# Experts of up to 32 rows on four column tiles of TensorE, their pairs in a chain of their own

## The chip, the cores and the metric

The kernel runs on 1 core of one Trainium2 chip. The metric is the device time of one execution in microseconds (us). Before the change it is 2599.8 us, the median of 3 runs (2597.35 to 2602.37).

## The reference, cut to what matters

Two transformer blocks run one after the other on 512 tokens of width 1024. The first holds differential attention, a gated linear recurrence and an MLP; the second holds sparse and forgetting attention and a mixture of 32 experts, of which each token takes four. The change is in the experts alone:

```
logits = (xf @ w_router + b_router).astype(jnp.float32)
top_v, top_i = lax.top_k(logits, TOP_K)
w = jax.nn.softmax(top_v, axis=-1)
...
sizes = jnp.bincount(flat_e, length=N_EXPERTS).astype(jnp.int32)
xs = xf[tok]
h = lax.ragged_dot(xs, w_up, sizes) + b_up[sorted_e]
g, lin = jnp.split(h, 2, axis=-1)
g = jnp.minimum(g, SWIGLU_LIMIT)
lin = jnp.clip(lin, -SWIGLU_LIMIT, SWIGLU_LIMIT)
act = g * jax.nn.sigmoid(SWIGLU_ALPHA * g) * (lin + 1.0)
y = lax.ragged_dot(act, w_down, sizes) + b_down[sorted_e]
y = y * w.reshape(-1)[order][:, None].astype(y.dtype)
return jax.ops.segment_sum(y, tok, num_segments=n).reshape(B, T, D)
```

An expert has 1024 x 2048 and 1024 x 1024 weights in fp32. With the reference's inputs the router gives the experts these numbers of rows, by size: 149, 143, 130, 127, 126, 121, 101, 101, 87, 87, 82, 74, then 63, 57, 53, 51, 45, 43, 43, 42, 40, 36, 33, and nine of 31, 30, 29, 29, 29, 26, 19, 12 and 9. The counts are known only at run time.

## The kernel before, in words

**Two ways to run an expert.** `expert` takes up to 128 rows: the rows and the weights are split into a high and a low part (`split`, ACT at L219 and DVE at L220), and TensorE multiplies three terms (`part`, bias at L1316, products at L1322). `few` takes up to 64 rows and multiplies fp32 weights as they come: `halves` cuts the 512 columns of a product into two halves that land on partitions 0 to 63 and 64 to 127 of one bank (biases L1517, products L1521). The rows are gathered by POOL (L1289), turned by TensorE (`flip`, L1303) and copied to `xf` by DVE (L1307) or split; the activation is `gated` (L1345 to L1349). In a few it is turned back at L1550 and copied at L1551 into `h`, which lies in the tile `y`. `finish` scales the result into the same tile `y` (ACT at L1364 for an expert; ACT at L1369 and DVE at L1370 for a few), and POOL adds it to the output by a scatter (L1293).

**The weights.** Each expert's weights are 12 chunks of 1 MB (`ORDER`: eight of w_up, four of w_dn), read by SP's queue (L1122) into a ring of eight buffers (`RAW`). A chunk's buffer is refilled with the chunk eight places on when it has been read: after the products in a few, after the split in an expert.

**The order at run time.** The experts are sorted by size on the chip (`order`) and their number and places are read from a table (`ovi`) by `load` (L1214). A pair is a small expert by `few` and then a big one by `expert`, so that the weights of one come while TensorE works at the other; the small ones are paired smallest first. `pairs` nests fifteen branches (L1235), each with one pair in it, and runs on to `rest`, which bisects (L1243, L1247) to the fews that have no big partner. There are 11 pairs with these inputs and then nine fews and one more. A branch not taken jumps over all the code of the deeper ones.

**The second rows.** In the first four pairs (`SECOND`) the big expert also runs its rows beyond 128, up to 32 of them, on four column tiles of 32 rows: `second_rows` turns them (L1459), `second` multiplies (biases L1476, products L1482). In those pairs the weights stay in the ring until both have read them.

In the expert the order of the work is written out as follows (`finish` is called by the expert for the few ahead of it):

```
for i in range(12):
    n = e * 12 + i
    if i < 10:
        self.split(*self.pairs[(n + 2) % self.PAIRS], self.raw(n + 2))
        ...
    self.part(bank(i), x if i < 8 else m["h"], i, self.pairs[n % self.PAIRS], one)
    if two:
        for k in range(i + (i > 0), min(i + 2, 12)):
            self.second(k, e)
            self.refill(e * 12 + k)
    if i == 0 and e:
        self.finish(e - 1, False)
```

The scheduler then sets the order on each engine's queue. Names of tiles: `lg` and `mm` are PSUM banks of the products, `pv` those of the second rows, `tr` of the transposes; `b` is any of several buffers, `wh` and `wl` the high and low part of a chunk.

Of the kernel before, what the change touches and what calls it, by code (L numbers as in the profile page):

```python
# [11 lines left out]
F32 = mybir.dt.float32  # L12
# [4 lines left out]
AF = mybir.ActivationFunctionType  # L17
OP = mybir.AluOpType
# [7 lines left out]
NE, TT = 32, 128  # L26
# [131 lines left out]
class K:  # L158
# [1050 lines left out]
    def places(self, srt):  # L1209

        tc, nc = self.tc, self.nc

        def load(i, n):
            return nc.values_load(self.ovi[0:1, i:i + 1], min_val=0, max_val=n, skip_runtime_bounds_check_because="a count")  # L1214

        plain = load(2, 1)
        with tc.If(plain > 0) as cmp:
            self.expert(0)
        with cmp.Else():
            kind, nfar = load(0, 1), load(7, 64)  # L1220
            with tc.If(kind > 0) as cm2:
                self.expert(0)
            with cm2.Else():
                self.few(0)
            with tc.If(nfar > 0):
                self.extra(srt)
                with tc.For_i(0, nfar, 1) as it:
                    er = nc.values_load(self.li[0:1, ds(it, 1)], engines=(mybir.EngineType.SP, mybir.EngineType.DVE),
                                        min_val=0, max_val=NE - 1, skip_runtime_bounds_check_because="an expert's number")
                    self.far(er, it)  # L1230
        nP = load(1, 15)

        def pairs(t):
            if t < NE // 2 - 1:
                with tc.If(nP > t):  # L1235
                    self.few(1 + 2 * t, True, t < self.SECOND)
                    self.expert(2 + 2 * t, t < self.SECOND)
                    pairs(t + 1)

        def rest(lo, hi):  # L1240
            if hi - lo > 1:
                mid = (lo + hi) // 2
                with tc.If(nP < mid):  # L1243
                    rest(lo, mid)
# [110 lines left out]
            return mm[(s + i // 2) % 4]  # L1355
        return mm[(s + i % 2) % 4]

    def finish(self, e, big):

        nc, m = self.nc, self.m  # L1360
        sl, i = m["sl"][e // 4 % 2], e % 4
        if big:
            for c in range(2):
                nc.scalar.activation(m["y"][0][:, 512 * c:512 * c + 512], self.bank(e, 8 + c), AF.Copy, scale=sl["w"][:, i:i + 1])  # L1364
            self.scatter(m["y"][0], sl, i)
        else:
            for c in range(2):
                p, w = self.bank(e, 8 + c), sl["w"][:64, i:i + 1]
                nc.scalar.activation(m["y"][0][:64, 512 * c:512 * c + 256], p[:64, :256], AF.Copy, scale=w)  # L1369
                nc.vector.tensor_scalar(m["y"][0][:64, 512 * c + 256:512 * c + 512], p[64:, :256], w, None, op0=OP.mult)  # L1370
            self.scatter(m["y"][0], sl, i, 64)

    def numbers(self, e):

# [41 lines left out]
    def expert(self, e, two=False):  # L1416

        nc, m = self.nc, self.m
        one, x, act = m["one"][e % 2], m["x"][e % 2], m["act"][0]
        bank = partial(self.bank, e)  # L1420
        self.numbers(e)
        if two:
            self.second_rows()
# [4 lines that stand above are left out]
                if not two:  # L1428
                    self.refill(n + 2)
            if i < 2 and not two:  # L1430
                self.refill(n)
# [13 lines left out]
        self.finish(e, True)  # L1445

    def cut(self, w, up, j, n, of):

# [56 lines left out]
    def halves(self, p, x, i, e):  # L1505
# [5 lines left out]
        o = p[:64, :256], p[64:, :256]  # L1511

        cut = lambda w, n: self.cut(w, up, j, n, 2)
        if up and kh == 0:
            b = self.bup.bitcast(F32)[:, 512 * (j // 2):512 * (j // 2) + 512]
            for n in range(2):
                nc.tensor.matmul(o[n], self.m["one"][e % 2].bitcast(F32)[:, j % 2, :64], cut(b, n), start=True, stop=False)  # L1517
        w = self.raw(e * 12 + i).rearrange("p (k f) -> p k f", k=4)
        for k in range(4):
            for n in range(2):  # L1520
                nc.tensor.matmul(o[n], x(4 * kh + k), cut(w[:, k], n), start=not up and kh == k == 0, stop=kh == 1 and k == 3)  # L1521

    def few(self, e, paired=False, second=False):

        nc, m = self.nc, self.m
        self.numbers(e)
        xf, act = m["xf"], m["act"][0][:, :512]
        hf = m["y"][0][:, :512].rearrange("p (t a r) -> p t a r", t=4, a=2)
        h = lambda k: hf[:, k % 2, k // 2] if k < 4 else hf[:, k % 2 + 2, k // 2 - 2]
        for i in range(12):  # L1530
            n = e * 12 + i
            self.halves(self.bank(e, i), (lambda k: xf[:, k]) if i < 8 else h, i, e)
            self.refill(n)
            if i > 9 and (paired or e == NE - 1):
                self.unfold(n + 2)
            if i == 0 and e and e % 2 == 0:
                self.finish(e - 1, False)
            self.ahead(e, i, 8, paired)
            if i == 3 and second:
                self.further(e + 1)  # L1540
            if i in (3, 5, 7):
                j = i // 2
                pg, pl = [self.bank(e, k)[:, :256] for k in (0, 2)] if j == 1 else \
                    [self.bank(e, i)[:, 128 * k:128 * k + 128] for k in range(2)]
                self.gated(pg, pl, self.side(act, j, 64))
            if i in (5, 8, 9):
                t0, t1 = {5: (0, 2), 8: (2, 3), 9: (3, 4)}[i]
                p = self.tr()
                for t in range(t0, t1):
                    nc.tensor.transpose(p[:, t - t0], act[:, 128 * t:128 * t + 128], self.ident)  # L1550
                nc.vector.tensor_copy(hf[:, t0:t1].rearrange("p t a r -> p t (a r)"), p[:, :t1 - t0])  # L1551
            if e == NE - 1 and i == 6:
                self.last_rows(e)
        if e % 2 == 0:
            self.finish(e, False)
        if e == NE - 1:
            self.last(e)

# [176 lines left out]
    def order(self, c):  # L1735


        nc, m, ones = self.nc, self.m, self.c["ones"]
# [10 lines left out]
        gt = S2[:, 160:222].rearrange("p (a e) -> p a e", a=2)  # L1749
        col = [S2[:, 284 + i:285 + i] for i in range(12)]  # L1750
        kc, big, q1, g, sb, far, ex = col[:7]
        r4 = S2[:, 296:298]
        r, na = [r4[:, i:i + 1] for i in range(2)]
# [45 lines left out]
        v.memset(of[:, 3:7], 0.0)  # L1799
# [139 lines left out]
```

## Time and profile before

| what | value |
| --- | --- |
| time, median of 3 runs | 2599.8 us (2597.35 to 2602.37) |
| profiled execution, its own time | 2600.15 us |
| its span | 2598.1 us (2.05 us lie around it) |
| mean granted TensorE clock | 0.972 |
| PE busy | 2425.4 us, 93% |
| DVE busy | 1326.2 us, 51% |
| ACT busy | 1043.5 us, 40% |
| POOL busy | 174.5 us, 7% |
| HBM read over the span | 530.03 MB |

The shares are averages over stages with different limits. The expert stage begins in the 22nd of the 40 slices and ends in the 39th. A window's line gives the busy time of each engine in it, the granted clock of TensorE as a share of full speed, and the mean busy share of the 16 DMA engines. In a timeline the bracket behind an instruction tells how long its engine was idle before it, and what released it; "q" behind an engine is its sequencer, which issues DMAs and runs branches.

### The profile page before, as it was taken

How to read it: one execution, taken by the hardware profiler on the slowest of the kernel's cores; microseconds unless marked ns; L12 is line 12 of the kernel's file. 1: busy time of each engine (PE TensorE's matmuls, PEld its weight loads, DVE VectorE, ACT ScalarE, POOL GpSimd, SP SyncE). 2: the span in 40 equal slices, each digit the busy share in tenths (PEclk: the TensorE clock that was granted, in tenths of full speed). 3: DMA queues.
4: the chain of work that ended last, by engine and by line, in shares of the span. 5: the costliest groups of instructions: out<-in, count | busy, mean ns of one | idle time of the engine just before them, and what ended most of it. 6: DMA issues, size and time to landing. Idle time of an engine off the chain costs nothing. (4 is left out here: it accounts for less than half of the span.)

```text
span 2598.1 us, 41846 instructions
## 1 busy us (share of the span) xinstructions
PE 2425.4 (93%) x17042; PEld 1941.2 (75%) x17042; DVE 1326.2 (51%) x2473; ACT 1043.5 (40%) x1578; POOL 174.5 (7%) x184
## 2 busy tenths in 40 slices
PE   7999999999999999999989999999999999788888
PEld 5789987898898898898976676666666666554557
DVE  6767753344333344557585466445656666121135
ACT  5755552223223324557353344334444444111133
POOL 0021100000000000000010010110001000000000
PEclk9999999999999999999979999999999999899999
DMA  4122222322222222220378889989999999799990
GB/s 160 65 90 78 74 70 89 127 86 88 98 93 86 98 70 83 75 71 17 109 271 324 305 317 333 341 301 367 381 378 392 385 403 373 294 399 400 407 376 33
DMA packets 86474, 552.63 MB, mean 213 GB/s; under 512 B 11799, under 2 KB 12951, under 8 KB 24936
## 3 DMA queue, kind: packets, MB, share of 16 engines
q1 hardware_dynamic: 71280, 508.33, 50.6%
q0 software_dynamic: 8352, 29.76, 4.7%
q10 hardware_dynamic: 6616, 11.53, 1.3%
q8 instruction: 142, 2.33, 0.4%
q14 instruction: 84, 0.69, 0.1%
HBM read 530.03 MB, written 19.55 MB: 212 GB/s over the span
## 5 line engine op out<-in xcount | busy, mean ns | idle before, releaser
L245 PE MATMUL mm<-b,wh 128*128 128x512 f32 (+1 forms) x1840 | 512.8, 365 | 1.7 <-ACT b L222 0.8
L245 PEld LDWEIGHTS mm<-b,wh 128*128 128x128 f32 x1840 | 328.8, 190 | 65.4 <-issue 3.4
L245 PE MATMUL mm<-b,wl 128*128 128x512 f32 (+2 forms) x920 | 335.2, 365 | 1.3 <-DVE wl L205 1.3
L245 PE MATMUL mm<-wh,b 128*128 128x256 f32 x1488 | 284.3, 287 | 1.5 <-DVE b L675 0.8
L205 DVE TENSOR_TENSOR wl<-raw,wh 128x2048 fp32r<-128x2048 f32 x81 | 185.5, 2290 | 176.2 <-ACT wh L204 176.2
L204 ACT ACTIVATE wh<-raw 128x2048 fp32r<-128x2048 f32 x81 | 155.1, 1915 | 261.2 <-PE mm L245 248.8
L245 PEld LDWEIGHTS mm<-wh,b 128*128 128x128 f32 x1488 | 235.9, 191 | 4.6 <-DVE b L675 1.2
L245 PE MATMUL mm<-wl,b 128*128 128x256 f32 x744 | 213.0, 286 | 1.0 <-DVE wl L205 1.0
L220 DVE TENSOR_TENSOR wl<-b,wh 128x2048 fp32r<-128x2048 f32 x74 | 169.2, 2288 | 65.4 <-ACT wh L219 62.4
L245 PEld LDWEIGHTS mm<-b,wl 128*128 128x128 f32 (+1 forms) x920 | 174.6, 190 | 31.8 <-DVE wl L205 2.2
L1521 PE MATMUL lg<-b,xf 128*64 128x256 f32 x1280 | 154.3, 389 | 14.7 <-DMA b<-w_up 10.1
L219 ACT ACTIVATE wh<-b 128x2048 fp32r<-128x2048 f32 x74 | 141.0, 1908 | 61.8 <-DMA b<-w_up 30.8
L245 PEld LDWEIGHTS mm<-wl,b 128*128 128x128 f32 x744 | 141.9, 191 | 2.5 <-DVE wl L205 1.3
L1521 PEld LDWEIGHTS lg<-b,xf 128*64 128x64 f32 x1280 | 94.3, 139 | 65.7 <-DMA b<-w_up 15.9
L1521 PE MATMUL lg<-b,b 128*64 128x256 f32 x1024 | 130.7, 394 | 7.5 <-DMA b<-w_dn 7.2
L213 POOL TENSOR_TENSOR rs<-rm,c_nhalf 128x1 f32<-128x1 f32 (+3 forms) x52 | 53.0, 1021 | 1158.9 <-DVE rm L211 1150.6
L1521 PEld LDWEIGHTS lg<-b,b 128*64 128x64 f32 x1024 | 76.0, 141 | 49.1 <-issue 11.5
L1345 ACT ACTIVATE sg<-mm,seven 128x128 f32<-128x128 f32 (+2 forms) x48 | 21.8, 455 | 223.2 <-PE mm L1521 180.9
L1521 PE MATMUL mm<-pp,xf 128*64 128x256 f32 x640 | 84.3, 388 | 4.6 <-DMA pp<-w_up 4.5
L1347 DVE SCALAR_TENSOR_TENSOR sg<-lg,sg 128x256 f32<-128x256 f32 (+1 forms) x48 | 19.2, 399 | 127.6 <-ACT sg L1346 127.6
L1521 PE MATMUL mm<-b,xf 128*64 128x256 f32 x640 | 74.8, 383 | 7.0 <-DMA b<-w_up 7.0
L1345 ACT ACTIVATE sg<-lg,seven 128x256 f32<-128x256 f32 (+1 forms) x48 | 21.7, 452 | 146.1 <-PE lg L1521 118.4
(534 smaller groups left out, 4597.9 us busy)
## 6 DMA issues: line engine op xcount, KB each, us to landing
b<-w_up SPq DMA_DIRECT2D x190, 1024.0 KB, 6.7
b<-w_dn SPq DMA_DIRECT2D x96, 1024.0 KB
pp<-w_up SPq DMA_DIRECT2D x64, 1024.0 KB, 13.4
raw<-w_in SPq DMA_DIRECT2D x39, 1024.0 KB, 4.9
pp<-w_dn SPq DMA_DIRECT2D x32, 1024.0 KB, 14.2
raw<-w_up SPq DMA_DIRECT2D x16, 1024.0 KB, 5.8
raw<-w_down SPq DMA_DIRECT2D x16, 1024.0 KB, 4.8
raw<-w_out SPq DMA_DIRECT2D x8, 1024.0 KB, 4.8
```

Source lines behind the costliest of these rows:

```text
L204: nc.scalar.activation(wh, raw, AF.Copy)
L205: nc.vector.tensor_tensor(wl, raw, wh.bitcast(F32), op=OP.subtract)
L213: self.nc.gpsimd.tensor_tensor(r, m, self.c["nhalf"][:, :n], op=OP.pow)
L219: nc.scalar.activation(hi, src, AF.Copy)
L220: nc.vector.tensor_tensor(lo, src, hi.bitcast(F32), op=OP.subtract)
L245: self.nc.tensor.matmul(ps, l, r, start=(i == 0), stop=(i == n - 1))
L1345: nc.scalar.activation(sg, pg, AF.Relu, scale=-1.0, bias=m["seven"][:rows, 0:1])
L1347: nc.vector.scalar_tensor_tensor(sg, pg, 7.0, sg, op0=OP.min, op1=OP.mult)
L1521: nc.tensor.matmul(o[n], x(4 * kh + k), cut(w[:, k], n), start=not up and kh == k == 0, stop=kh == 1 and k == 3)
```

## The change

`halves` becomes `pieces` with the number of column tiles `of`, and `few`, `expert` and `finish` take `of` too. With `of` = 4 a few has 32 rows: four column tiles of 32 partitions and 128 columns, two transposes of the activation instead of four, and a scatter of 32 rows. The table gets one more count, `nT`: the number of pairs whose small expert has at most 32 rows; it is nine with these inputs. A chain `tiny` of fifteen nested branches holds the pairs with `of` = 4. Behind it the count of pairs is loaded, and a bisection holds the pairs with `of` = 2 that are at or beyond `nT`: two of them here. `rest` stays.

```
-        nP = load(1, 15)
-
-        def pairs(t):
+        nT = load(3, 15)
+
+        def pair(t, of):
+            self.few(1 + 2 * t, True, t < self.SECOND, of)
+            self.expert(2 + 2 * t, t < self.SECOND, of)
+
+        def tiny(t):
             if t < NE // 2 - 1:
-                with tc.If(nP > t):
-                    self.few(1 + 2 * t, True, t < self.SECOND)
-                    self.expert(2 + 2 * t, t < self.SECOND)
-                    pairs(t + 1)
+                with tc.If(nT > t):
+                    pair(t, 4)
+                    tiny(t + 1)
+
+        def pairs(lo, hi):
+            if hi - lo > 1:
+                mid = (lo + hi) // 2
+                with tc.If(nT < mid):
+                    pairs(lo, mid)
+                with tc.If(nP > mid):
+                    pairs(mid, hi)
+            else:
+                with tc.If(nT < lo + 1):
+                    with tc.If(nP > lo):
+                        pair(lo, 2)
...
-        pairs(0)
+        tiny(0)
+        nP = load(1, 15)
+        pairs(0, NE // 2 - 1)
         rest(0, NE // 2 - 1)
```

The finish, the products and the few (lines that only pass `of` on are left out):

```
+        rows, y = 128 // of, m["y"][0]
+        w = sl["w"][:rows, i:i + 1]
+        for c in range(2):
+            for g in range(of):
+                p, o = self.bank(e, 8 + c)[rows * g:rows * g + rows, :512 // of], y[:rows, 512 * c + 512 // of * g:][:, :512 // of]
+                if g % 2:
+                    nc.vector.tensor_scalar(o, p, w, None, op0=OP.mult)
+                else:
+                    nc.scalar.activation(o, p, AF.Copy, scale=w)
+        self.scatter(y, sl, i, rows)
...
-                self.finish(e - 1, False)
+                self.finish(e - 1, of)
...
         for k in range(4):
-            for n in range(2):
-                nc.tensor.matmul(o[n], x(4 * kh + k), cut(w[:, k], n), start=not up and kh == k == 0, stop=kh == 1 and k == 3)
-
-    def few(self, e, paired=False, second=False):
+            for g in range(of):
+                nc.tensor.matmul(o[g], x(4 * kh + k), self.cut(w[:, k], up, j, g, of), start=not up and kh == k == 0,
+                                 stop=kh == 1 and k == 3)
+
+    def few(self, e, paired=False, second=False, of=2):
...
+        rows, q = 128 // of, 4 // of
+        xf, act = m["xf"], m["act"][0][:, :1024 // of]
...
-                t0, t1 = {5: (0, 2), 8: (2, 3), 9: (3, 4)}[i]
+                t0, t1 = {5: (0, q), 8: (q, q + 1), 9: (q + 1, 2 * q)}[i]
```

And in `order`:

```
+        v.tensor_scalar(gt[:, 2], key[:, 1:], 32 * 32 + 31.5, None, op0=OP.is_lt)
...
         v.tensor_tensor(nP, q1, na, op=OP.min)
+        v.tensor_tensor(of[:, 3:4], nP, tiny, op=OP.min)
```

The order of the instructions moves at three places. On PE, in the second pair (pair 1), at the end of the few and the start of the expert; before (b_12234 is `y` with h or the second rows, L1521 the few's products, `xg` the gathered rows):

```order
L1303 MATMUL tr<-c_ident,xg 128x128 x4
L1550 MATMUL tr<-c_ident,b_12234 128x128
L1521 MATMUL lg<-b_12225,b_12234 64x256 x8
L1303 MATMUL tr<-c_ident,xg 128x128 x4
L1550 MATMUL tr<-c_ident,b_12234 128x128
L1521 MATMUL lg<-b_12343,b_12234 64x256 x16
L1459 MATMUL tr<-c_ident,b_12234 128x32 x8
L1316 MATMUL mm<-bup,one_12237 128x512
L1322 MATMUL mm<-wh,b_12232 128x512
L1322 MATMUL mm<-wl,b_12232 128x512
```

and now:

```order
L1476 MATMUL tr<-c_ident,b_12234 128x32 x4
L1333 MATMUL mm<-bup,one_12237 128x512
L1493 MATMUL pv<-bup,one_12237 32x128
L1476 MATMUL tr<-c_ident,b_12234 128x32 x4
L1537 MATMUL lg<-b_12345,b_12234 32x128 x16
L1493 MATMUL pv<-bup,one_12237 32x128 x7
L1333 MATMUL mm<-bup,one_12237 128x512
L1333 MATMUL lg<-bup,one_12237 128x512 x2
L1499 MATMUL pv<-b_12206,xs 32x128 x16
L1339 MATMUL mm<-wh,b_12232 128x512
L1499 MATMUL pv<-b_12206,xs 32x128 x13
L1339 MATMUL mm<-wl,b_12232 128x512
```

The products of the second rows (`pv`, L1499 now) stand beside the first product with `wh`, ahead of the first with `wl`; before they stood further down, behind the first chunk's products; the few's products (`lg`) still end ahead of the expert's first.

On ACT, in the same pair, before:

```order
L1346 ACTIVATE sg<-sg,seven 128x128
L219 ACTIVATE b_12232<-tr 128x512
L219 ACTIVATE wh<-b_12206 128x2048
L219 ACTIVATE b_12232<-tr 128x512
L219 ACTIVATE wh<-b_12206 128x2048
L1369 ACTIVATE b_12234<-lg,s0w 64x256 x2
L219 ACTIVATE raw<-pp 128x2048
```

and now:

```order
L1363 ACTIVATE sg<-sg,seven 128x64
L219 ACTIVATE b_12232<-tr 128x512 x2
L1387 ACTIVATE b_12234<-lg,s0w 32x128 x4
L219 ACTIVATE wh<-b_12206 128x2048 x2
L219 ACTIVATE raw<-pp 128x2048
```

Both splits of the flipped rows and the few's finish (L1387 now) stand ahead of the splits of the expert's chunks; the second flip and the finish (L1369) stood behind one and two of them.

On PE, behind the last nested branch, before:

```order
L1322 MATMUL mm<-raw,h 128x512 x10
L1322 MATMUL mm<-b_12224,h 128x512 x12
L1235 UNCONDITIONAL_BRANCH x16
L1243 COMPARE_AND_BRANCH x3
L1247 COMPARE_AND_BRANCH
L1517 MATMUL lg<-bup,one_12238 64x256 x2
```

and now, where the tiny chain ends (the branches to `rest` follow the other pairs):

```order
L1339 MATMUL mm<-b_12224,h 128x512 x12
L1239 UNCONDITIONAL_BRANCH x16
L1214 TENSOR_LOAD ovi
L1246 COMPARE_AND_BRANCH x3
L1251 COMPARE_AND_BRANCH
L1252 COMPARE_AND_BRANCH
```

The chain's end, a load of a count and the branches of a bisection come twice on the way now: once behind the ninth pair and once (without the load) behind the eleventh. The order of SP's refills and of POOL's gathers and scatters is the same in both.

## Rows read from the trace of the kernel before

**Rows 1.** The page's slices: the span in 40 equal parts, busy tenths.

```profile
DMA  4122222322222222220378889989999999799990
```

**Rows 2.** Windows by pair: us; PE, PEld, DVE, ACT, POOL busy; PEclk, DMA share, GB/s.

```profile
1467.41:1550.93 83.52, 79.44 (x816) 56.84 (x815) 45.42 (x74) 35.98 (x43) 8.53 (x7) 0.98 0.88 324
1550.93:1637.33 86.40, 84.21 (x831) 57.68 (x830) 48.48 (x93) 36.04 (x43) 7.22 (x7) 0.96 0.87 314
1637.33:1721.18 83.85, 80.27 (x815) 57.52 (x815) 45.59 (x74) 36.04 (x43) 8.58 (x7) 0.96 0.87 323
...
1794.00:1864.06 70.06, 64.59 (x386) 45.85 (x385) 40.72 (x52) 32.67 (x33) 6.81 (x4) 0.98 0.99 381
...
2214.80:2226.92 12.12, 0.00 (x0) 0.03 (x1) 0.29 (x1) 0.69 (x1) 1.60 (x1) 0.62 0.47 102
2226.92:2282.58 55.66, 53.18 (x441) 37.72 (x443) 10.34 (x31) 6.45 (x15) 3.30 (x3) 0.93 0.88 345
2282.58:2348.16 65.58, 55.88 (x458) 32.99 (x456) 15.07 (x56) 6.92 (x16) 4.75 (x4) 0.97 1.02 400
```

**Rows 3.** Windows in pair 1, PE alone: us, PE busy, PEclk, DMA share, GB/s.

```profile
1491.00:1497.00 6.00, 1.92 (x21) 1.00 1.00 414
1497.00:1503.00 6.00, 6.00 (x52) 0.72 1.01 420
1503.00:1551.00 48.00, 48.00 (x547) 1.00 0.81 306
```

**Rows 4.** Timeline of ACT in pair 1: start, us, instruction, idle before and releaser.

```profile
1491.84 1.91 ACT L219 ACTIVATE wh<-b 128x2048 fp32r<-128x2048 f32 x1 [4.86 <-DMA b<-w_up]
...
1495.99 0.81 ACT L1369 ACTIVATE b<-lg,s0w 64x256 f32<-64x256 f32 x2
```

**Rows 5.** The list of waits: us in total, times, longest.

```profile
ACT wh L219 <- DMA b<-w_up: 30.8, 11, 4.9
```

**Rows 6.** Timeline of PE in pairs 0 and 1: products and biases, two chunks each.

```profile
1419.08 2.12 PE L1482 MATMUL pv<-b,xs 128*32 128x128 f32 x64
1432.09 0.43 PE L1476 MATMUL pv<-bup,one 128*32 128x128 f32 x8
...
1467.41 0.65 PE L1517 MATMUL lg<-bup,one 128*64 128x256 f32 x4
1467.89 3.62 PE L1521 MATMUL lg<-b,xf 128*64 128x256 f32 x32
```

**Rows 7.** Timeline of PE in pair 1, from the few to the expert.

```profile
1488.95 3.70 PE L1521 MATMUL lg<-b,b 128*64 128x256 f32 x32
1496.73 0.68 PE L1459 MATMUL tr<-c_ident,b 32*128 32x32 f32 x8 [4.08 <-DVE b L220]
...
1498.26 0.63 PE L1322 MATMUL mm<-wl,b 128*128 128x512 f32 x1
```

**Rows 8.** Timeline of DVE in pair 1, the split of the expert's first chunk.

```profile
1493.78 2.29 DVE L220 TENSOR_TENSOR wl<-b,wh 128x2048 fp32r<-128x2048 f32 x1 [4.42 <-ACT wh L219]
```

**Rows 9.** Timeline of PE in pairs 0 and 2: the few's last products, inside the expert.

```profile
1414.16 2.81 PE L1521 MATMUL lg<-b,b 128*64 128x256 f32 x24
...
1582.36 4.69 PE L1521 MATMUL lg<-b,b 128*64 128x256 f32 x24
```

**Rows 10.** Timeline of SP's queue in pair 1: issues of refills.

```profile
1469.83 5.94 SPq L1122 DMA_DIRECT2D b<-w_dn  x4
1477.93 2.06 SPq L1122 DMA_DIRECT2D b<-w_up  x2
```

**Rows 11.** Timeline of DVE in pair 3: the few's first copy of h.

```profile
1651.16 0.42 DVE L1551 COPY b<-tr 128x256 f32<-128x256 f32 x1 [4.26 <-DMA acc<-b,s1i]
```

**Rows 12.** The page's DMA queues: packets, MB, share of 16 engines' span.

```profile
q0 software_dynamic: 8352, 29.76, 4.7%
```

**Rows 13.** Timeline of PE behind the last pair: the gap's end and the first few.

```profile
2226.92 1.12 PE L1517 MATMUL lg<-bup,one 128*64 128x256 f32 x4 [12.12 <-DVE one L1286]
2229.47 6.25 PE L1521 MATMUL lg<-b,xf 128*64 128x256 f32 x32 [1.43 <-SPq L1243]
```

More of the change, by code (lines that the diff above doesn't have):

```diff
@@ L1356, in bank, with finish @@
         return mm[(s + i % 2) % 4]
-    def finish(self, e, big):
+    def finish(self, e, of=2):
         nc, m = self.nc, self.m
         sl, i = m["sl"][e // 4 % 2], e % 4
[L1362 to L1371, printed above, removed]
+        rows, y = 128 // of, m["y"][0]
[8 more added lines that the diff above has]
+        self.scatter(y, sl, i, rows)
     def numbers(self, e):
@@ L1414, in last, with expert @@
             self.split(self.y[0][:64, cc], self.y[1][:64, cc], y)
-    def expert(self, e, two=False):
+    def expert(self, e, two=False, of=2):
         nc, m = self.nc, self.m
@@ L1444, in expert @@
             self.second_finish()
-        self.finish(e, True)
+        self.finish(e, 1)
     def cut(self, w, up, j, n, of):
@@ L1503, in second_finish, with pieces @@
         self.scatter(m["actb"][0], m["sl"][2], 0, 32)
-    def halves(self, p, x, i, e):
+    def pieces(self, p, x, i, e, of):
         nc = self.nc
@@ L1510, in halves @@
         kh, j = (c % 2, c // 2) if up else ((i - 8) // 2, 0)
-        o = p[:64, :256], p[64:, :256]
-        cut = lambda w, n: self.cut(w, up, j, n, 2)
+        r = 128 // of
+        o = [p[r * g:r * g + r, :512 // of] for g in range(of)]
         if up and kh == 0:
             b = self.bup.bitcast(F32)[:, 512 * (j // 2):512 * (j // 2) + 512]
-            for n in range(2):
-                nc.tensor.matmul(o[n], self.m["one"][e % 2].bitcast(F32)[:, j % 2, :64], cut(b, n), start=True, stop=False)
+            for g in range(of):
+                nc.tensor.matmul(o[g], self.m["one"][e % 2].bitcast(F32)[:, j % 2, :r], self.cut(b, up, j, g, of), start=True, stop=False)
         w = self.raw(e * 12 + i).rearrange("p (k f) -> p k f", k=4)
         for k in range(4):
-            for n in range(2):
-                nc.tensor.matmul(o[n], x(4 * kh + k), cut(w[:, k], n), start=not up and kh == k == 0, stop=kh == 1 and k == 3)
-    def few(self, e, paired=False, second=False):
+            for g in range(of):
+                nc.tensor.matmul(o[g], x(4 * kh + k), self.cut(w[:, k], up, j, g, of), start=not up and kh == k == 0,
+                                 stop=kh == 1 and k == 3)
+    def few(self, e, paired=False, second=False, of=2):
         nc, m = self.nc, self.m
         self.numbers(e)
-        xf, act = m["xf"], m["act"][0][:, :512]
-        hf = m["y"][0][:, :512].rearrange("p (t a r) -> p t a r", t=4, a=2)
-        h = lambda k: hf[:, k % 2, k // 2] if k < 4 else hf[:, k % 2 + 2, k // 2 - 2]
+        rows, q = 128 // of, 4 // of
+        xf, act = m["xf"], m["act"][0][:, :1024 // of]
+        hf = m["y"][0][:, :2 * q * 128].rearrange("p (t a r) -> p t a r", t=2 * q, a=of)
+        h = lambda k: hf[:, k % q + q * (k // 4), k % 4 // q]
         for i in range(12):
             n = e * 12 + i
-            self.halves(self.bank(e, i), (lambda k: xf[:, k]) if i < 8 else h, i, e)
+            self.pieces(self.bank(e, i), (lambda k: xf[:, k, :rows]) if i < 8 else h, i, e, of)
             self.refill(n)
@@ L1536, in few @@
             if i == 0 and e and e % 2 == 0:
-                self.finish(e - 1, False)
+                self.finish(e - 1)
             self.ahead(e, i, 8, paired)
@@ L1542, in few @@
                 j = i // 2
-                pg, pl = [self.bank(e, k)[:, :256] for k in (0, 2)] if j == 1 else \
-                    [self.bank(e, i)[:, 128 * k:128 * k + 128] for k in range(2)]
+                w = 256 // of
+                pg, pl = [self.bank(e, k)[:, :2 * w] for k in (0, 2)] if j == 1 else [self.bank(e, i)[:, w * k:w * k + w] for k in range(2)]
                 self.gated(pg, pl, self.side(act, j, 64))
             if i in (5, 8, 9):
-                t0, t1 = {5: (0, 2), 8: (2, 3), 9: (3, 4)}[i]
+                t0, t1 = {5: (0, q), 8: (q, q + 1), 9: (q + 1, 2 * q)}[i]
                 p = self.tr()
@@ L1550, in few @@
                     nc.tensor.transpose(p[:, t - t0], act[:, 128 * t:128 * t + 128], self.ident)
-                nc.vector.tensor_copy(hf[:, t0:t1].rearrange("p t a r -> p t (a r)"), p[:, :t1 - t0])
+                if t1 > t0:
+                    nc.vector.tensor_copy(hf[:, t0:t1].rearrange("p t a r -> p t (a r)"), p[:, :t1 - t0])
             if e == NE - 1 and i == 6:
@@ L1554, in few @@
         if e % 2 == 0:
-            self.finish(e, False)
+            self.finish(e)
         if e == NE - 1:
@@ L1748, in order @@
         key, t32, P, P2 = [S2[:, o:o + n] for o, n in ((0, 32), (32, 32), (64, 32), (96, 64))]
-        gt = S2[:, 160:222].rearrange("p (a e) -> p a e", a=2)
+        gt = S2[:, 160:253].rearrange("p (a e) -> p a e", a=3)
         col = [S2[:, 284 + i:285 + i] for i in range(12)]
         kc, big, q1, g, sb, far, ex = col[:7]
-        r4 = S2[:, 296:298]
-        r, na = [r4[:, i:i + 1] for i in range(2)]
+        r4 = S2[:, 296:299]
+        r, na, tiny = [r4[:, i:i + 1] for i in range(3)]
         of = self.ovf
@@ L1798, in order @@
         v.tensor_copy(of[:, 8:40], pe[:, :NE])
-        v.memset(of[:, 3:7], 0.0)
+        v.memset(of[:, 4:7], 0.0)
         v.tensor_copy(self.ovi, of)
```

## The prediction

> **What bounds the kernel now.** I read the page's slices first. The expert stage runs from 1385 us to about 2500 us, and in it DMA is at eight to nine tenths, against two to three before [rows 1]. So the question in each pair (a few, then an expert) is whether TensorE or the weight stream ends it. The table of windows by pair splits the eleven pairs into two kinds [rows 2]. Pairs 0 to 3, which also carry the second rows (pairs 1 to 3 stand there), last about 84 to 86 us, with PE busy for 79 to 84 us and DMA at 0.87 to 0.88. The other seven are like pair 5: 70 us, PE 65 us, DMA 0.99; the fews of the last stage reach 1.02 at 400 GB/s, which I take as full. The early pairs are bound by PE, the later ones by the stream.
>
> Inside a pair the stretches differ again. In pair 1 PE is busy 1.92 of 6 us shortly before the expert's first split product, and 48.00 of 48 us from 1503 us to the pair's end [rows 3]. What ends that idle time is not the few: ACT's split of the expert's first chunk waits for that chunk's DMA [rows 4], and the list of waits has this in all 11 pairs, 30.8 us in sum [rows 5]. So the few's products lie in the shade of the stream, and in pairs 0 to 3 only what stands behind the landing on PE counts.
>
> **The change part by part.** All is summed against the profiled execution, 2600.15 us (0.35 us over the median of the runs).
>
> *Products of the nine tiny fews.* 32 products of 64 rows (two chunks) take 3.62 us and a pair of biases 0.65 us; 64 of 32 rows take 2.12 us and their biases 0.43 us, as the second rows of the same pairs show [rows 6]. A few of 12 chunks and four biases costs 12 x 1.81 + 1.3 = 23.0 us now and 12 x 1.06 + 0.9 = 13.6 us then: 9.4 us less PE work in a few, 85 us in nine. By the trace nearly all of it is cover: the chunk that the expert's first split waits for has landed at 1491.84 us, 24.4 us after the pair's start [rows 4], so shorter products turn into PE idle time. The Trainium skill ("TensorEngine Tiling (Array Packing)", section "Theoretical Speedup") gives up to 2x for 64 rows and up to 4x for 32, so halved products, where the rows show 3.62 to 2.12 us; by that rule the nine fews would lose 9 x 11.5 = 104 us of PE work, and the sum would be 2509 us if each microsecond of it counted.
>
> *Term 1, pairs 0 to 3, behind the landing.* Five parts:
> - In odd pairs the transposes of the second rows wait 4.08 us on PE for DVE's split of the flipped rows [rows 7], which DVE does behind the chunk's split. The product with wl could start when DVE has written it, at 1493.78 + 2.29 = 1496.07 us [rows 8], and starts at 1498.26 [rows 7]. In the new order the flips stand ahead of the chunk's split. 2.2 us in two pairs: -4.4.
> - In even pairs 24 of the few's last products run inside the expert, 2.81 us in pair 0 and 4.69 in pair 2 [rows 9]. They end ahead of the landing then: -7.5.
> - The second rows' first two chunks, 2.12 us [rows 6], move ahead of the first wl product, into idle time: 4 x 2.1 = -8.4.
> - The stream starts earlier. The few's first refill issues at 1469.83 us, 2.4 us after the pair's start [rows 10]; with faster products at about 1.3. The refill of the expert's first chunk issues at 1477.93 [rows 10] and lands 14 us later, behind chunks issued ahead of it, so I give it about the first one's 1 us. Against that, ACT now does the few's finish ahead of the split (four pieces). I take half: 4 x 0.5 = -2.
> - The clock. Behind the idle window the granted clock is 0.72 for 6 us [rows 3], which costs 6 x 0.28 = 1.7 us. With PE idle for longer I take 1.5 us more a pair: +6.
>
> Sum -16. Bounds: -31 (no clock loss, and the landing 2.2 us earlier in each pair) and -8 (the second rows don't fit the idle time).
>
> A wait limits the few's earlier end: its first transposed h is copied into the y tile, which the previous expert's scatter still reads; that copy waited 4.26 us for the scatter in pair 3, until 1651.16 [rows 11], 13.8 us after its start at 1637.33 [rows 2]. Chunks 8 to 11 also come just ahead of the expert's first. I place a tiny few's end between 17 and 23 us.
>
> *Term 2, pairs 4 to 8.* PE gains the same, but the stream is full. The scatter of a tiny few writes 32 rows instead of 64. The software queue spends 4.7% of 2598 us on 8352 packets [rows 12], 14.6 ns each; 32 rows at one or two packets are 0.5 to 0.9 us. I take -1 a pair, and +1 for the clock in all: -4. Bounds: -10 (each pair at a share of 1.02 in place of 0.99, 2.1 us of 70) and +3 (a slow stretch of 0.6 us each and nothing else).
>
> *Term 3, the second chain.* After pair 8 every engine leaves the tiny chain, reloads the pairs' count and takes three jumps before pair 9, as it does today once, before the last stage; that boundary stays. Today's shows PE idle for 12.12 us, then biases at 1.12 us instead of 0.65, first products at 6.25 instead of 3.62 [rows 6] and a wait of 1.43 [rows 13]: 12.1 + 3.1 + 1.4 = 16.6. Part comes back, since the ring is full by then: the two fews behind it last 55.66 us, the next two 65.58 [rows 2]. From the side of the stream, 12.12 us at 0.47 instead of 1.02 are 6.5 us lost and 55.66 us at 0.88 are 7.6: 14 us. Nothing hides it, as no engine issues past the jumps. With the load and the table's two added vector operations, under 1 us, I take +13, bounds +8 and +17.
>
> Sum: -16 - 4 + 13 = -7: 2593 us, 0.3% under the runs.
>
> At nothing I cost the refills on SP and the gathers on POOL, whose order is unchanged; the few's scatter, which POOL starts some 10 us earlier beside the stream (its transfer is term 2's); and the eight pieces of a finish in place of four, hidden while it ends ahead of the landing.
>
> **The rivals.**
> - *Slower: the finish holds up the split.* ACT does the few's finish ahead of the expert's first split. If the few ends as late as pair 1's does now, 1488.95 + 3.70 = 1492.65 [rows 7], 25.2 us in, and four pieces take twice the 0.81 us of today's two [rows 4], the split starts 26.8 us in, not 24.4. It decides from a finish that ends past the landing. Pairs 0 to 3 then give 4 x 2.4 - 4.4 - 7.5 - 8.4 + 6 = -5 and lose the -2; pairs 4 to 8, whose split frees the ring later too, +1 a pair: 2600 - 5 + 5 + 13 = 2613, or 2607 with pairs 4 to 8 untouched; 2609 as a middle. For it speaks the wait for the y tile [rows 11]; against it, products that are half as long behind that wait.
> - *No change.* The second rows don't fit (-8.4 gone), the stream gives nothing, the clock stays as now, term 2 is 0: -12 + 13 = +1, 2601. For it speaks DMA at 1.00 in the idle stretch [rows 3].
> - *Much faster.* The first chunk's landing follows its issue, 10.5 us in now and 10.5 x 13.6 / 23.0 = 6.2 then, 4.3 us earlier: 3.8 us more than in the sum in four pairs, and term 2 at its bound: 2593 - 15 - 6 = 2572. Against it stands a stream at 1.00 ahead of the landing [rows 3]; for it, 0.87 over the early pairs.
> - *All PE time counts.* Nine fews at 9.4 us, 85 us, less the boundary's 13: 2528. The page on array packing would give it (the Trainium skill, as cited above). DMA at 0.99 speaks against it in five of the nine.
> - *The change doesn't act:* if no pair counts as tiny (the router's counts decide at run time), only a boundary is left: 2613.
>
> **How the numbers follow.** The forecast has 0.46 (its own range 2580 to 2600), slower 0.22, no change 0.17, much faster 0.11, all PE time and no effect 0.02 each. A measurement here tells about 0.2%, 5.2 us, from no change, so faster ends at 2594.6: some 0.35 of the forecast's 0.46 and the two fast rivals, 0.48. The rest of the forecast and the no-change rival are 0.28. Slower is 0.24. The range from 2570 to 2611 holds the forecast, no change, most of the slower rival and half of the much faster one.
>
> **What would show it.** In the changed profile: PE busy 13 to 14 us with a tiny few's products; ACT's first split still released by the DMA, 22 to 24 us after the pair's start; longer PE idle time before it and a slow clock behind; pairs 0 to 3 at 77 to 81 us, pairs 4 to 8 at 68 to 72; a second gap of about 12 us after the ninth pair. I am wrong if that split waits for the finish's pieces, if the landing moves by over 2 us, or if the gap after the ninth pair is under 5 us or over 20.

## The result and the profile after

The changed kernel takes 2622.7 us (median of 6 runs, 2613.9 to 2629.0) beside 2597.2 us for the one before: a ratio of 1.0091 over all executions (not of the two medians), 95% interval 1.0066 to 1.0116. It is slower, where 2593 us and slightly faster were forecast, and outside the range of 2570 to 2611 us. The profiled execution took 2623.86 us, with a span of 2622.1 us against 2598.1.

The windows by pair of the changed kernel (us; PE, PEld, DVE, ACT, POOL busy; PEclk, DMA share, GB/s). The line from 2010.55 us is pair 8 with the new boundary behind it, the last is pair 10 with the old one:

```profile
1391.50:1472.86 81.36, 77.19 (x1036) 55.73 (x1036) 47.60 (x97) 35.33 (x45) 6.74 (x6) 0.94 0.88 324
1472.86:1553.81 80.95, 72.64 (x1022) 54.27 (x1021) 44.35 (x76) 35.64 (x45) 7.12 (x7) 0.96 0.90 334
1553.81:1639.77 85.96, 76.81 (x1038) 55.55 (x1037) 47.03 (x94) 35.67 (x45) 7.14 (x7) 0.92 0.86 315
1639.77:1718.67 78.90, 71.98 (x1022) 53.84 (x1021) 44.44 (x76) 35.99 (x45) 7.14 (x7) 0.98 0.92 343
1718.67:1795.81 77.14, 62.31 (x608) 45.42 (x607) 40.92 (x63) 32.36 (x35) 5.42 (x5) 0.87 0.91 348
1795.81:1866.06 70.25, 59.36 (x591) 45.30 (x591) 40.20 (x53) 32.68 (x35) 4.88 (x4) 0.90 0.98 380
...
2010.55:2099.97 89.42, 62.23 (x608) 45.46 (x607) 40.74 (x59) 33.04 (x36) 6.48 (x5) 0.84 0.84 313
...
2168.93:2252.76 83.83, 65.29 (x402) 45.01 (x401) 41.50 (x58) 33.06 (x34) 6.58 (x5) 0.96 0.90 337
```

PE's work did shrink: 76.81 us in pair 2 where 84.21 stood [rows 2]. But its length is 85.96 us against 86.40, so the idle time took the place of the work. By stretches, against the same windows of before:

| stretch | before, us | after, us | difference |
| --- | --- | --- | --- |
| up to pair 0 | 1385.4 | 1391.5 | +6.1 |
| pairs 0 to 3 | 335.8 | 327.2 | -8.6 |
| pairs 4 to 7 | 282.1 | 291.9 | +9.8 |
| pair 8 and what lies behind it | 70.6 | 89.4 | +18.8 |
| pairs 9 and 10 with the old boundary | 153.1 | 152.8 | -0.3 |
| from there to the end | 371.2 | 369.3 | -1.8 |

The first line is no part of the change: pair 0 starts between 1380.6 and 1391.5 us in the profiles of the kernels below, in no order that follows an edit. The other lines say three things: the early pairs gained half of what was forecast, the stream-bound pairs lost, and pair 8 with the new boundary takes 18.8 us more.

The list of waits of the changed kernel (us in total, times, longest) shows what is new:

```profile
DVE b L1570 <- DMA acc<-b,s0i: 34.6, 4, 11.3
DVE b L1570 <- DMA acc<-b,s1i: 34.3, 4, 10.7
PE tr L1860 <- DVE oh L1858: 24.0, 5, 7.4
...
ACT wh L219 <- DMA b<-w_up: 5.5, 6, 2.0
```

DVE's first copy of h (L1570, before at L1551) waits for the previous expert's scatter 68.9 us in eight pairs; before it was 15.6 us in three. And ACT's waits for a chunk's DMA before a split are 5.5 us, where they were 30.8 us [rows 5]; none of them stands at the first split of one of the nine tiny pairs: something else comes last there. Pair 4 shows the chain. On DVE:

```profile
1733.59 0.29 DVE L1570 COPY b<-tr 128x128 f32<-128x128 f32 x1 [9.42 <-DMA acc<-b,s0i]
...
1734.52 1.39 DVE L1858 TENSOR_SCALAR oh<-iotab,posx 128x128 bf16<-128x128 bf16 x8
```

On PE, in the same pair:

```profile
1734.83 0.19 PE L1860 MATMUL tr<-rwt,oh 128*128 128x6 bf16 x1 [6.53 <-DVE oh L1858]
1734.94 0.64 PE L1537 MATMUL mm<-pp,xf 128*32 128x128 f32 x4
...
1746.89 1.08 PE L1537 MATMUL lg<-b,b 128*32 128x128 f32 x32
```

On ACT:

```profile
1748.04 0.80 ACT L1387 ACTIVATE b<-lg,s0w 32x128 f32<-32x128 f32 x2 [0.94 <-PE lg L1537]
1749.31 0.36 ACT L1387 ACTIVATE b<-lg,s0w 32x128 f32<-32x128 f32 x1 [0.47 <-DVE b L1385]
1749.58 3.69 ACT L219 ACTIVATE wh<-b 128x2048 fp32r<-128x2048 f32 x2
```

The copy stands until 14.9 us after the pair's start, and with it all that is queued behind it on DVE, among that the comparisons (L1858) for the next experts' slots. Most of these stand in every second few; on PE their transposes (L1860) lie between the few's products, and PE waits 6.53 us for them here (7.4, 6.5, 5.1 and 3.3 us in pairs 2, 4, 6 and 8), though the products right behind them read `xf` and need nothing of the copy. In pairs 1 and 3 the few's last products wait for the copy itself, 6.3 and 4.6 us. The few's last group of products starts 28.2 us in, the pieces of its finish follow, and only then does ACT split the expert's first chunk, 30.9 us in. In pair 1 before, it did so 24.4 us in, as soon as the chunk had landed [rows 4].

The copy waits for longer not only because the few is ahead of its old time. In pairs 5 to 8 POOL issues the scatter 1.1 us after the pair's start in both kernels, but it lands 12.2 to 13.0 us in where it landed 10.2 to 10.4 us in before. What lengthens it was not tested.

Behind the wait TensorE's clock is low as well. Windows of PE in pair 4 (us, PE busy, PEclk, DMA share, GB/s) of the changed kernel:

```profile
1728.00:1734.00 6.00, 0.30 (x6) 0.65 1.04 323
1734.00:1740.00 6.00, 5.17 (x40) 0.50 1.02 392
1740.00:1746.00 6.00, 6.00 (x104) 0.71 1.01 418
```

and of the kernel with h apart (below), at the same work in the first two lines and at the expert's first products in the third:

```profile
1704.00:1710.00 6.00, 5.68 (x100) 1.00 1.02 322
1710.00:1716.00 6.00, 5.76 (x113) 1.00 1.03 339
...
1722.00:1728.00 6.00, 4.47 (x10) 0.50 1.02 402
```

Behind the idle stretch the granted clock is 0.50, the lower of the two levels (1.2 of 2.4 GHz), then 0.71, where the few's remaining products run; without the wait it stays at 1.00 there. It falls to 0.50 later in that pair, behind the wait for the expert's first split, and the pair's mean clock is 0.90 beside 0.87. What the slow clock alone costs was not told apart from the wait.

### The profile page after: what moved, and what is told of

It reads as the page before. It is cut to its first block, busy times and chain, and to the rows that moved or that the text cites. A ratio compares the mean times of both kernels' runs of the same rounds, so it can differ in the third digit from the quotient of the medians.

```text
span 2622.1 us, 45733 instructions
## 1 busy us (share of the span) xinstructions
PE 2373.1 (91%) x18896; PEld 1928.2 (74%) x18896; DVE 1317.8 (50%) x2484; ACT 1042.7 (40%) x1596; POOL 168.9 (6%) x184
## 3 DMA queue, kind: packets, MB, share of 16 engines
q0 software_dynamic: 8064, 28.58, 4.2%
## 5 line engine op out<-in xcount | busy, mean ns | idle before, releaser
L219 ACT ACTIVATE wh<-b 128x2048 fp32r<-128x2048 f32 x74 | 139.2, 1902 | 17.6 <-DMA b<-w_ple 9.3
L1537 PE MATMUL lg<-b,xf 128*32 128x128 f32 (+1 forms) x1856 | 127.3, 322 | 14.2 <-DMA b<-w_up 10.0
L1537 PE MATMUL lg<-b,b 128*32 128x128 f32 (+1 forms) x1600 | 108.1, 336 | 23.6 <-DVE b L1570 14.9
L1362 ACT ACTIVATE sg<-mm,seven 128x64 f32<-128x64 f32 (+3 forms) x48 | 20.9, 435 | 260.4 <-PE mm L1537 182.6
L1537 PEld LDWEIGHTS lg<-b,xf 128*32 128x32 f32 (+1 forms) x1856 | 87.0, 123 | 46.0 <-DMA b<-w_up 15.9
L1537 PEld LDWEIGHTS lg<-b,b 128*32 128x32 f32 (+1 forms) x1600 | 72.4, 130 | 45.9 <-DVE b L1570 16.4
L1537 PE MATMUL mm<-pp,xf 128*32 128x128 f32 (+1 forms) x928 | 84.7, 340 | 11.6 <-DMA pp<-w_up 5.9
L1570 DVE COPY b<-tr 128x128 f32<-128x128 f32 (+1 forms) x51 | 16.2, 318 | 133.7 <-PE tr L1568 54.9
L1339 PE MATMUL mm<-wh,b 128*128 128x512 f32 x192 | 72.4, 447 | 4.8 <-ACT wh L219 4.8
```

The source lines that it names most:

```text
L219: nc.scalar.activation(hi, src, AF.Copy)
L1339: nc.tensor.matmul(p, s[:, kk], w[:, k], start=not up and kk == j == 0, stop=kk == KC - 1 and j == len(terms) - 1)
L1362: nc.scalar.activation(sg, pg, AF.Relu, scale=-1.0, bias=m["seven"][:rows, 0:1])
L1537: nc.tensor.matmul(o[g], x(4 * kh + k), self.cut(w[:, k], up, j, g, of), start=not up and kh == k == 0, stop=kh == 1 and k == 3)
```

## The experiments

Each was timed against the kernel before on the same chip; a ratio below 1 is faster than before. Differences between two versions are taken from their ratios; for versions of different sessions they have no interval of their own.

**The changed kernel once more**, for comparison with the runs of its session.

> The changed kernel as it is, on the chip of the next three runs and against the same runs of before, so that the parts can be compared: 20 to 28 us over before, as measured first. If the four tiles (4 us over before, with a single chain) and the chain (10 us over before, with two tiles) simply added up it would be 14 us over before.

Measured: 2621.9 us beside 2600.8, ratio 1.0066 (1.0042 to 1.0090), so 11 to 23 us, less than at first and than the 20 to 28 expected. The two figures of this kernel overlap between 1.0066 and 1.0090. The sum of the parts, 1.0035 and 1.0014 below, is 1.0049, inside this interval but not inside the first one: what the two parts do to each other can't be told from these runs.

**The chain alone**, with two column tiles in it.

```
-                    pair(t, 4)
+                    pair(t, 2)
```

> The second chain stays, and its pairs use two column tiles as before: chain, loads and table without the four tiles. Theory (the boundary costs what the one ahead of the last stage does): 13 to 17 us, 2610 to 2615 us, with PE idle for 12 to 14 us behind the ninth pair. Rival (the loss is all in the tiny fews, jumps are hidden by the full ring): within 4 us of before, 2593 to 2601.

Measured: 2613.5 us beside 2603.2, ratio 1.0035 (1.0016 to 1.0053), 4 to 14 us, short of most of the 13 to 17 expected. The profiled execution took 2623.8 us, 10 more than the median. The gap behind pair 8 (timeline of PE), and the windows of pair 8 with the gap and of pair 9:

```profile
2080.85 2.96 PE L1339 MATMUL mm<-b,h 128*128 128x512 f32 x12
2099.17 1.12 PE L1533 MATMUL lg<-bup,one 128*64 128x256 f32 x4 [15.36 <-DVE one L1303]
2100.05 4.73 PE L1537 MATMUL lg<-b,xf 128*64 128x256 f32 x32
```

```profile
2011.60:2099.17 87.57, 67.50 (x401) 47.15 (x401) 41.59 (x58) 33.07 (x34) 6.59 (x5) 0.90 0.87 326
2099.17:2167.04 67.87, 65.51 (x385) 47.35 (x385) 40.70 (x52) 32.19 (x32) 5.19 (x3) 0.95 0.94 374
```

PE stands for 15.36 us, and pair 8 with the gap is 17.0 us longer than the 70.6 of before. The rival, jumps hidden by the full ring, falls, though the timing's lower end comes close to its 4 us; the price of about 9 us lies in the range that the prediction took from the old boundary, 8 to 17.

**The four tiles alone**, in a single chain, fixed for these inputs.

```
-                with tc.If(nT > t):
-                    pair(t, 4)
+                with tc.If(nP > t):
+                    pair(t, 4 if t < 9 else 2)
...
-        nP = load(1, 15)
-        pairs(0, NE // 2 - 1)
```

> Four column tiles in pairs 0 to 8 of a single chain as before, the nine fixed for these inputs: the tiles without the second chain. Theory (both the wait for y and the boundary cost): the changed kernel less 13 to 19 us, 2604 to 2610 us, still 5 to 13 us slower than before. Rival (the boundary is free): within 4 us of 2623. Rival (the tiles are worth what was forecast and the chain costs all): 2575 to 2582.

Measured: 2607.6 us beside 2603.2, ratio 1.0014 (0.9997 to 1.0030), so 1 us faster to 8 slower, where 5 to 13 slower were expected. The tiles alone save nothing, though PE's busy time is 49.8 us less (2375.6 us against 2425.4). That is less than the prediction's 85 us; between the starts of pairs 0 and 9 the mean granted clock is 0.91 here and 0.98 before, so each product is busy for longer.

**h out of y.**

```
-        hf = m["y"][0][:, :2 * q * 128].rearrange("p (t a r) -> p t a r", t=2 * q, a=of)
+        hf = m["act"][0][:, 512:512 + 2 * q * 128].rearrange("p (t a r) -> p t a r", t=2 * q, a=of)
```

> The few's turned activation h is kept in the unused half of the tile act, not in y, which the previous expert's scatter still reads. Nothing else changes. Theory (the wait for y): in the changed kernel DVE's first copy of h waits 68.9 us in 8 of the 9 tiny pairs for that scatter's landing, and DVE's queue with it; without it that wait is gone, a tiny few ends 17 to 22 us after the pair's start instead of 22 to 31, the expert's first split is released by its chunk's DMA again, pairs 4 to 8 come back to 68 to 71 us each and pairs 0 to 3 to 75 to 79: 20 to 30 us less than the changed kernel, 2593 to 2603 us. Rival (the loss is the slow clock behind longer PE idle time, and the second chain): PE idles as long without the wait, the pairs stay within 1 us and the time within 5 us of 2623.

Measured: 2591.9 us beside 2603.2, ratio 0.9966 (0.9949 to 0.9984): faster than before with the second chain still in it. ACT has the same order of instructions in the nine pairs as in the changed kernel, and PE and DVE have the same but for a few near ones that change places. DVE's wait for the scatter is gone from the list, and the copy in pair 4 comes 7.5 us after the pair's start instead of 14.9 (timeline of DVE):

```profile
1704.84 0.29 DVE L1570 COPY b<-tr 128x128 f32<-128x128 f32 x1 [1.97 <-PE tr L1568]
```

Windows of pairs 2 and 4, and of pair 8 with its gap:

```profile
1540.28:1619.16 78.88, 75.10 (x1038) 55.01 (x1037) 47.24 (x94) 36.05 (x45) 7.17 (x7) 0.98 0.91 344
...
1697.36:1767.56 70.20, 61.77 (x608) 46.28 (x607) 41.54 (x63) 32.94 (x35) 5.42 (x5) 0.90 1.00 387
...
1977.51:2067.24 89.73, 65.05 (x607) 48.02 (x607) 41.22 (x59) 33.28 (x36) 6.49 (x5) 0.81 0.84 312
```

Pairs 0 to 3 take 316.8 us in sum, pairs 4 to 7 280.2: 10.4 and 11.7 us less than in the changed kernel. Pair 8 and its gap stay at 89.7 us. The rival by clock alone falls; pairs 4 and 7 still have a mean clock of 0.90 and last 70.2 us, at a DMA share of 1.00 and 0.97.

**Both together: one chain and h apart.**

> Both edits: a single chain with four tiles in its first nine pairs, fixed for these inputs, and h out of the tile y. Theory: the two losses add up, so 2575 to 2587 us, 10 to 20 us faster than before. Rival (the fews' time is hidden by the stream in any case, and a clock loss comes on top): 2595 to 2605.

Measured: 2578.1 us beside 2603.2, ratio 0.9905 (0.9878 to 0.9933), 17 to 32 us faster, at or above the 10 to 20 expected. With h apart the single chain is worth 0.0061 more than the two chains, 16 us.

**h apart in the kernel before.**

> The kernel before with h in the unused half of act: does the wait for y cost anything there? It is 15.6 us in three pairs, and in all eleven the split waits for the DMA afterwards. Theory (hidden by the stream): within 4 us of before. Rival (part of what h apart gives the changed kernel has nothing to do with the tiles): 6 to 15 us faster.

Measured: 2599.9 us beside 2600.8, ratio 1.0002 (0.9987 to 1.0017). The wait for y costs nothing that shows there (3 us less to 4 more). It became a cost by what the change shortened.

**The finish two chunks later.** This was to take the finish from ahead of the split.

```
-            if i == 0 and e:
+            if i == 2 and e:
                 self.finish(e - 1, of)
```

> The changed kernel with the few's finish handed to ACT and DVE two chunks later in the expert, so that the pieces that wait for the few's last products no longer stand ahead of the first split; h stays in y. If the split is late because ACT's finish stands ahead of it (the slower rival of the prediction), it is released by its chunk's DMA again, 22 to 25 us after the pair's start in all nine pairs, and most of the loss goes: 12 to 20 us less than the changed kernel. If the loss is the few itself, whose last products stand ahead of the expert's first on PE and end 22 to 31 us in because DVE waits for y, less than 6 us goes.

Measured: 2645.9 us beside 2600.8, ratio 1.0168 (1.0147 to 1.0190): slower still. It tells nothing of the question. ACT's order changed in pairs 0 to 3 only, and there for two of the four pieces; in pair 4 all four stand ahead of the split as they did, and it still starts 30.2 us in. And in pairs 0 to 3 the finish now follows the second rows' first activation, which lies in y too, so these kernels compute something else for part of those rows, and a new wait for the scatter comes up on DVE, in the middle of the expert:

```profile
1443.88 0.22 DVE L1365 TENSOR_SCALAR b<-pv 128x64 f32<-128x64 f32 x1 [6.18 <-DMA acc<-b,s0i]
```

All the loss is there: pairs 0 to 3 last 354.9 us in sum, pairs 4 to 7 293.3, as in the changed kernel.

**The same with h apart**, with the same edit to the finish.

> Both: h out of y and the finish two chunks later. With h apart the split still waits for the finish in six pairs (it starts 23.7 to 26.6 us in). Theory: it then starts at 22.5 to 24.5, the four early pairs gain 1 to 2 us each, the later ones nothing, as they are bound by the stream: 4 to 8 us less than with h apart alone, 16 to 20 us faster than before. Rival (PE's few ends late all the same, for the gather of the second rows): within 2 us of h apart alone.

Measured: 2624.2 us beside 2600.8, ratio 1.0082 (1.0054 to 1.0110). It too has its loss in pairs 0 to 3 (345.7 us), while pairs 4 to 7 stay at 281.5.

**The split ahead of the finish**, by telling the scheduler to issue the finish behind the first split:

```
-                self.finish(e - 1, of)
+                with self.tc.issue_after(self.first.ins):
+                    self.finish(e - 1, of)
...
             if i > 9 and (paired or e == NE - 1):
                 self.unfold(n + 2)
+                if i == 10:
+                    first = self.cast
```

> The changed kernel with the few's finish issued behind ACT's split of the expert's first chunk, where the scheduler had put it ahead; h stays in y. Theory (DVE's wait for y makes the few late, and the finish hands that on to the split): the split is released by its chunk's DMA at 22 to 25 us in all nine pairs, but the few's last products, still late, stand ahead of the expert's first on PE: about 4 us in each of the six late pairs comes back, 10 to 20 us less than the changed kernel. Rival of the prediction alone (the finish's place is the whole loss): 25 us or more, as fast as with h apart. Rival (the finish's place costs nothing): less than 4 us.

Measured: 2601.4 us beside 2598.9, ratio 1.0004 (0.9992 to 1.0017), so 16 to 23 us less than the changed kernel's two ratios. That is nearly all that the changed kernel lost, though not all that h apart regains. The wait for y is all there, 78.1 us in the list, and PE's order keeps the few's late products ahead of the expert's. The split waits for its DMA in pairs 3, 5 and 7 alone, not in all nine as expected: in the other six it starts right behind ACT's copy of the flipped rows (L219 too), and that waits for transposes which stand among the few's late products on PE. In pair 4 (timeline of ACT) it starts 27.2 us in:

```profile
1729.00 0.60 ACT L219 ACTIVATE b<-tr 128x512 fp32r<-128x512 f32 x1 [1.47 <-PE tr L1320]
1729.50 1.90 ACT L219 ACTIVATE wh<-b 128x2048 fp32r<-128x2048 f32 x1
```

The windows of pairs 2 and 4:

```profile
1541.66:1624.89 83.23, 74.36 (x1037) 54.71 (x1037) 47.09 (x94) 35.46 (x45) 8.95 (x7) 0.92 0.88 324
1702.26:1775.86 73.60, 59.90 (x608) 44.86 (x607) 40.67 (x63) 32.26 (x35) 9.33 (x5) 0.91 0.97 365
```

These are 85.96 and 77.14 in the changed kernel, 78.88 and 70.20 with h apart.

**Both orders right.**

> The same order with h apart. With h apart alone the split starts 24.5 to 26.6 us in in pairs 0 to 3 and 26.1 in pair 8, where its chunk has landed at about 23.5. Theory: the first wl product comes 1 to 3 us earlier in these five pairs, 5 to 12 us less than with h apart alone. Rival (the stream and the second rows' gather set the pairs): within 3 us of it.

Measured: 2586.2 us beside 2598.9, ratio 0.9945 (0.9926 to 0.9965), 0.0021 or 5 us better than h apart alone, at the lower end of what was expected; the two intervals overlap, so this gain is not settled. On ACT the split is now the first, waits for its DMA and nothing else, and the finish comes behind it (pair 4):

```profile
1714.72 1.91 ACT L219 ACTIVATE wh<-b 128x2048 fp32r<-128x2048 f32 x1 [3.14 <-DMA b<-w_up]
1716.54 0.59 ACT L1387 ACTIVATE b<-lg,s0w 32x128 f32<-32x128 f32 x2
```

Pairs 0 to 3 take 310.1 us in sum, pairs 4 to 7 279.4.

**One of two whole chains**, chosen at run time, so that it holds for any counts:

```
+        nT, nP = load(3, 15), load(1, 15)
...
+                with tc.If(nP > t):
+                    pair(t, 4 if t < four else 2)
+                    pairs(t + 1, four)
...
+        with tc.If(nT > 8) as cm3:
+            pairs(0, 9)
+        with cm3.Else():
+            pairs(0, 0)
```

> h apart, and instead of a tiny chain followed by another one of two whole chains: if at least nine pairs are tiny (known at run time), a chain whose first nine pairs have four tiles and the rest two; else a chain with two tiles in all. The boundary in the middle of the pairs goes, one more jump over the other chain comes at the end. Theory (the boundary costs 14 to 17 us, a jump about 4): 10 to 13 us less than with h apart alone, 17 to 25 us faster than before. Rival (a longer jump costs as much as three): within 3 us of h apart alone.

Measured: 2582.2 us beside 2598.9, ratio 0.9926 (0.9911 to 0.9941), 10 us better than with the two chains in a row, as expected. The gap in the middle is gone; the one at the end, with one more jump over the other chain in it, has grown from 12.12 us [rows 13] to:

```profile
2214.66 1.12 PE L1522 MATMUL lg<-bup,one 128*64 128x256 f32 x4 [18.75 <-DVEq L1246]
```

**All three edits**, the version with the lowest ratio.

> All three: h apart, the split ahead of the finish, either chain. If they add up 25 to 35 us faster than before; if the stream takes the split's gain back, 17 to 25.

Measured: 2576.4 us beside 2598.9, ratio 0.9898 (0.9880 to 0.9917), 22 to 31 us faster than before, which leaves open whether the parts add up in full (25 to 35). Windows of pairs 2, 4 and 8:

```profile
1542.19:1620.45 78.26, 74.23 (x1037) 55.25 (x1036) 47.53 (x94) 35.71 (x45) 8.94 (x7) 0.96 0.92 345
...
1698.49:1768.07 69.58, 62.38 (x608) 46.80 (x607) 40.95 (x63) 32.62 (x35) 7.13 (x5) 0.88 1.00 385
1978.25:2048.02 69.77, 61.94 (x608) 46.55 (x607) 40.69 (x59) 32.55 (x35) 6.70 (x4) 0.88 0.98 382
```

## Why the prediction was wrong, step by step

- **What bounds the pairs** was right. With both orders right, pairs 4 to 7 end at 279.4 us against 282.1 with a DMA share of 0.96 to 1.00, whatever PE saves.
- **A reading that hid the sign.** The list's 11 waits for a chunk's DMA [rows 5] are not one in each of the 11 pairs: pair 3 has two of them and pair 4 none. In pair 4 of the kernel before, the copy of h waits for the scatter longest, and the split comes right behind ACT's copy of the flipped rows, 24.9 us in (timelines of DVE and ACT):

```profile
1737.34 0.42 DVE L1551 COPY b<-tr 128x256 f32<-128x256 f32 x1 [7.24 <-DMA acc<-b,s0i]
...
1745.59 0.60 ACT L219 ACTIVATE b<-tr 128x512 fp32r<-128x512 f32 x1 [1.61 <-PE tr L1303]
1746.08 1.90 ACT L219 ACTIVATE wh<-b 128x2048 fp32r<-128x2048 f32 x1
```

With h apart in the kernel before, that split waits for its DMA again, 24.0 us in. So the wait for y had reached the expert's split once already; the prediction read the 4.26 us of pair 3 and not these 7.24.

- **The step that failed** is "I place a tiny few's end between 17 and 23 us", and with it the finish's pieces costed at nothing, "hidden while it ends ahead of the landing". The few's last product ended 21.7 to 30.8 us in, past 24 in seven of nine pairs, and the split waited for the finish's pieces, the first of the prediction's own signs of being wrong. The wait for y was seen, but only the few's own products were put behind it. What the runs show in its place: the wait holds DVE's whole queue; in pairs 2, 4, 6 and 8 the comparisons for the slots are in it, whose transposes stand between the few's products on PE; and in pair 4 PE, idle for 6.5 us, then works at a clock of 0.50. The two experiments that undo it from either end, h apart and the split ahead, bring back 26 to 32 us and 16 to 23 us of the changed kernel's time by their ratios. The wait is not the whole of this step: with h apart the few ends 20.3 to 25.2 us in, still past 23 in five pairs. In pairs 1 and 2 PE then waits 3.9 and 1.7 us for the gather of the second rows, and the gathers were costed at nothing.
- **The slower rival** was the right mechanism with its point of decision ("a finish that ends past the landing"), at 0.22 and 2609 us. Its size was wrong: the split was to come 2.4 us later in four pairs and 1 us in five, 14.6 us in all. Against the kernel before it came 4.9, 2.9, 8.0, 1.3, 6.0, -0.3, 5.4, -0.1 and 6.5 us later, 34.4 us in all. With h apart 7.7 us of the 34.4 are left, so 26.7 went with the wait for y. With both orders right the splits come 41.2 us earlier in sum than in the changed kernel, and the nine pairs with their gap take 674.5 us instead of 708.5: most of a split's delay had gone into the time.
- **Term 1** (-16, bounds -31 to -8) gave -8.6 in the changed kernel. Its PE work did move out of the way: from the expert's first product with wl to the pair's end the four pairs take 197.6 us in sum in the changed kernel, 218.5 before, with no sign there of the clock's +6. But that first product came 12.2 us later in sum. With both orders right it comes 4.5 us earlier, and the four pairs give 310.1 - 335.8 = -25.7.
- **Term 2** (-4) became +9.8 in pairs 4 to 7 by the late split, and is -2.7 in these four when repaired. The scatter's packets were counted rightly: the page has 8064 in the software queue, 288 fewer than before, one for each of 9 x 32 rows. The queue's share fell from 4.7% of 2598 us [rows 12] to 4.2% of 2622 us, by the trace 10.5 us or 1.2 a pair. That the -1 a pair comes near it is luck: one of these packets takes over twice the 14.6 ns that it was worked out from.

```profile
q0 software_dynamic: 8064, 28.58, 4.2%
```

- **Term 3** (+13, 8 to 17) held: 4 to 14 us by the chain alone, 16 us by the single chain with h apart, from either side of 13. In the changed kernel the gap is 13.95 us:

```profile
2099.97 1.12 PE L1533 MATMUL lg<-bup,one 128*64 128x256 f32 x4 [13.95 <-DVE one L1303]
2100.85 5.83 PE L1537 MATMUL lg<-b,xf 128*64 128x256 f32 x32
```

- **All PE time counts** (2528 us) fell, as it was expected to: two chunks of products went from 3.62 [rows 6] to 1.93 us (timeline of PE in pair 4 of the changed kernel, below), and the tiles alone changed the time by 1.0014. The Trainium skill ("TensorEngine Tiling (Array Packing)", section "Theoretical Speedup") gives up to 2x for 64 rows and up to 4x for 32, so up to a halving; the trace has a factor of 1.9.

```profile
1718.91 1.93 PE L1537 MATMUL lg<-b,xf 128*32 128x128 f32 x64
```

What stays open is how the chain and the late fews add up: the two timings of the changed kernel differ by more than their parts can settle.

## What to carry to other kernels

When an engine's work on hidden ground is shortened, look for what that work had been covering: here a write into a tile that a transfer still read cost nothing that showed before and 26 to 32 us afterwards. Look in the old trace for a place where the wait already gets through, as in pair 4 here. Price such a wait by everything queued behind it on its engine and by the work of other engines that is woven into theirs, not by the step that waits. Where a scheduler sets the order by estimated times, the cheaper step may be moved ahead of the one that feeds the pipeline; check each engine's order for it, and pin the feeding step first.

## What the runs showed that was not expected

Executions of the changed kernel spread over 15 us (2613.9 to 2629.0), those of before over 8.5 in the same comparison; over 29 executions in another session those of before spread over 23 us, so this is not shown to be the change's. One more jump at the end, over the whole other chain, lengthened the gap from 12.12 to 18.75 us; whether the number of jumps or their reach does it was not tested. And in the stream-bound pairs a slow clock cost no time that shows: with all three edits pairs 4 to 8 ran at mean granted clocks of 0.85 to 0.93 and took 349.5 us, before at 0.95 to 1.00 and 352.7 us.
